# RWKV output projection by token groups in readout order, its first group with a pool and a bank of its own, in a two-layer hybrid backbone on one core

## Chip, cores and metric

The kernel runs on one core of one Trainium2 chip, as one launch. The metric is the device time of the launch in microseconds (us). The engines are named as in the profile: PE (TensorE matmul), PEld (its weight load), DVE (VectorE), ACT (ScalarE), POOL (GpSimd), SP (the engine that issues nearly all DMAs here). Each engine executes its own instructions in the order in which they stand in the program.

## What is computed

Two layers over 512 latent tokens of width 1024 and 256 context tokens. Layer 0 is grouped-query attention with a SwiGLU feed-forward, layer 1 a bidirectional RWKV-7 mixer with a SwiGLU feed-forward, then a final RMSNorm. The change lies in two places: where layer 0 begins, and between the RWKV scan and the last feed-forward. The reference of the latter, cut to what matters:

```python
mu = jnp.mean(wkv, axis=-1, keepdims=True)                # wkv: both scan directions added, (B, T, H, 64)
var = jnp.mean(jnp.square(wkv - mu), axis=-1, keepdims=True)
gn = ((wkv - mu) * lax.rsqrt(var + GN_EPS)).reshape(B, T, H * N) * ln_g + ln_b
bonus = sum(jnp.sum(r * k_d * r_k, axis=-1, keepdims=True) for k_d in k_dirs) * v
out = (gn + bonus.reshape(B, T, H * N)) * g               # g = sigmoid(...) @ g2
y = out @ wo
x = x + m[:, 2] * y
h2 = _rmsnorm(x, norm2_g[i]) * (1.0 + m[:, 4]) + m[:, 3]
x = x + m[:, 5] * _swiglu(h2, ffn_wg[i], ffn_wu[i], ffn_wd[i])
```

All products with large weights are done in three parts: operand and weight are split into a high part (a cast to fp32r) and a low part (the rest), and high·high, low·high and high·low are summed in PSUM.

## The kernel before

The program is written in a tile framework whose scheduler decides the order of the instructions on each engine from the code, the pools and the buffer counts. So a change in one stage can also turn the order in another.

The stages, in the profiled execution: layer 0 (its norm and the projection of queries, keys and values first), the RWKV projections, the scan in token chunks of 64 (roughly 1290 to 1784 us), the readouts, the output projection (1814 to 1860 us), the feed-forward (to about 2207 us), the final norm and the write of the output.

**The scan's loads.** For each head group and chunk, the scan's inputs are computed in an elementwise phase that loads `rt`, `kt`, `kk`, `AR`, `GA` (`L1034`, `L1096`, `L1097`) and writes `d_q`, `d_b`; the scan's steps load `Rb`, `T`, `Bs` (`L1269`, `L1245`, `L1256`). SP issues all of them in one row. An issue that waits for a free buffer holds up all issues behind it.

**Readouts.** `readout(g, i)` (`L1386` to `L1433`) is called for two head groups g = 0, 1 and i = 0 to 3. It handles 128 tokens, chunks 3-i and 4+i of the eight, since the forward and backward scans meet in the middle and give these chunks at the same time. It loads `yr` (the scan's results, `L1392`) and `vr` (`L1396`), adds the two directions (`L1401`), normalises (`L1403` to `L1414`, on DVE for g = 1), transposes `yr` and `vr` on PE (`pw`, `pvb`), multiplies tg by g2 on PE (`pgt`), and forms z and its high and low parts `oTh`, `oTl` (`L1427` to `L1433`). A call (g, 3) can begin only after the last scan step.

**Output projection.** `out_half` (`L264`) computes for half of the tokens (256 columns) the eight output tiles f: four blocks b, each loading two `wr` raws of 512 KB (`L249`) and covering f = 2b and 2b+1. For each f, two units `wu` (high part by ACT, `L239`; low part by DVE or POOL in turn, `L241`) give 24 matmuls `yps`; `add_gated` (`L258`, DVE) adds the result to `xT`, whose part is then written to `xd`. There are seven unit buffers (`UNITS`) and four raws (`RAWS`), shared by both halves and the feed-forward, and six PSUM banks for `yps`. The halves are tokens 0 to 255 and 256 to 511, so half 0 needs chunks 0 to 3, and thus every one of the eight readouts.

**Where layer 0 begins.** `xT` (tokens transposed, 3 MB) is built and written to `xd` by one DMA (`L560`) that stands on SP ahead of loads of `wraw` (weights of the first projection); modulation gives `tt`, `hh` (its high part, ACT `L558`), `hl` (its low part, DVE `L559`).

## Time and profile before

| | |
|---|---|
| three timed runs | 2244.11, 2254.23, 2256.9 us (median 2254.23) |
| the profiled execution | 2246.71 us |
| its span, first to last instruction | 2245.0 us |
| mean granted TensorE clock | 0.934 |
| PE busy | 2005.4 us (89% of the span) |
| DVE, ACT, POOL busy | 1638.5, 1138.0, 684.3 us |

The span and the time of the profiled execution differ by 1.7 us. The runs of one and the same program lie up to 12.8 us apart (0.6%). PE is busy nine tenths of the span, but the share differs much by stage, so that a change in a stage is read from that stage alone.

### The profile page before, as it was taken

Reading aid. Unit: us, or ns where it says so; the run is one execution under the profiler, and the core shown is the slowest. Engines: PE = TensorE matmul, PEld = TensorE weight load, DVE = VectorE, ACT = ScalarE, POOL = GpSimd, SP = SyncE. Lnnn points to the kernel's source line nnn. Section 1 sums busy time; section 2 is a strip of 40 time slices with the busy share of each in tenths; the row PEclk is TensorE's granted clock in tenths of the full one; section 3 lists DMA queues with packets and bytes.
Section 4 is the critical chain, followed back from the end, with each engine's and each line's share of the span. In section 5 each row is a group of like instructions: output and inputs, shape, how many; then the busy total and the mean of one; then the engine's idle time right before and its main releaser. Section 6 shows DMA issues by size and latency. Waiting matters only on the chain.

```text
span 2245.0 us, 43057 instructions
## 1 busy us (share of the span) xinstructions
PE 2005.4 (89%) x16566; PEld 1769.6 (79%) x16566; DVE 1638.5 (73%) x3119; ACT 1138.0 (51%) x2322; POOL 684.3 (30%) x564
## 2 busy tenths in 40 slices
PE   6998999898999999996988979766878687999998
PEld 4995555697999999995776957655767586899998
DVE  4565556668777677768566488699586678899997
ACT  5536566655333333335333665865765556444443
POOL 1120000126444434423133141221110415666661
PEclk7999999999999999997997989896999788999999
DMA  8106663353221222212226574774644654332331
GB/s 305 57 20 225 225 229 109 124 160 130 77 75 57 75 67 75 66 52 71 85 84 223 163 214 150 218 210 127 196 137 148 197 160 139 116 104 87 111 98 72
DMA packets 250076, 294.12 MB, mean 131 GB/s; under 512 B 36200, under 2 KB 176720, under 8 KB 249488
## 3 DMA queue, kind: packets, MB, share of 16 engines
q1 hardware_dynamic: 249152, 290.52, 41.8%
q8 instruction: 131, 2.15, 0.4%
q10 hardware_dynamic: 352, 0.60, 0.1%
q0 software_dynamic: 368, 0.26, 0.1%
q14 instruction: 73, 0.60, 0.1%
HBM read 228.40 MB, written 50.33 MB: 124 GB/s over the span
## 4 chain that ended last, share of the span: by engine, by line
PE 63%; DVE 15%; DMA 8%; issue 5%; ACT 4%; POOL 3%; SPq 1%; DVEq 0%; POOLq 0%; ACTq 0%
PE yps L445 13%; PE A L395 8%; PE B L395 5%; PE C L395 5%; PE yps L228 5%; PE po L747 3%; PE S L728 2%; PE PTp L742 2%; PE mps L126 2%; PE pj L228 2%; PE qps L595 2%; DVE wu L241 2%; PE qps L597 2%; PE qps L596 2%; PE pr L1337 2%
## 5 line engine op out<-in xcount | busy, mean ns | idle before, releaser
L445 PE MATMUL yps<-gh,wu 128*128 128x384 f32 (+2 forms) x1120 | 324.7, 346 | 0.0
L258 DVE SCALAR_TENSOR_TENSOR xT<-yps,modT,xT 128x384 f32<-128x384 f32 (+3 forms) x360 | 185.4, 537 | 125.6 <-PE yps L445 106.9
L239 ACT CAST wu<-wr 128x512 fp32r<-128x512 f32 x276 | 168.5, 620 | 172.0 <-PE A L395 55.9
L239 ACT CAST wu<-ws 128x512 fp32r<-128x512 f32 x176 | 109.2, 621 | 223.5 <-PE yps L445 62.1
L445 PEld LDWEIGHTS yps<-gh,wu 128*128 128x128 f32 x1120 | 202.5, 189 | 11.4
L241 POOL TENSOR_TENSOR wu<-wr,wu 128x512 fp32r<-128x512 f32 x86 | 123.3, 1434 | 236.1 <-ACT wu L239 212.4
L445 PE MATMUL yps<-gl,wu 128*128 128x384 f32 (+2 forms) x560 | 193.1, 345 | 0.0
L241 DVE TENSOR_TENSOR wu<-wr,wu 128x512 fp32r<-128x512 f32 x190 | 164.8, 872 | 14.5 <-ACT wu L239 14.1
L349 POOL TENSOR_TENSOR ws<-wr 128x512 f32<-128x512 f32 x88 | 129.5, 1477 | 147.7 <-DMA wr<-in_ffn_wg_dram 67.9
L241 DVE TENSOR_TENSOR wu<-ws,wu 128x512 fp32r<-128x512 f32 x111 | 138.3, 1247 | 20.8 <-ACT wu L239 20.7
L241 POOL TENSOR_TENSOR wu<-ws,wu 128x512 fp32r<-128x512 f32 x65 | 100.1, 1540 | 65.5 <-ACT wu L239 65.5
L228 PE MATMUL yps<-oTh,wu 128*128 128x384 f32 (+1 forms) x512 | 111.3, 309 | 1.1 <-ACT wu L239 1.0
L445 PEld LDWEIGHTS yps<-gl,wu 128*128 128x128 f32 x560 | 105.9, 189 | 4.3
L731 DVE TENSOR_REDUCE mx<-S 128x1 f32<-128x768 f32 (+1 forms) x96 | 74.7, 778 | 44.4 <-PE S L728 43.9
L1136 POOL TENSOR_SCALAR_AFFINE_SELECT GA<-GA 64x512 f32<-64x512 f32 x48 | 37.6, 783 | 199.4 <-ACT GA L1134 196.4
L395 PE MATMUL C<-x5h,wu 128*128 128x384 f32 (+1 forms) x352 | 85.2, 319 | 14.4 <-ACT x5h L312 12.3
L743 ACT COPY PT<-PTp 128x384 f32<-128x384 f32 (+1 forms) x160 | 69.4, 466 | 54.0 <-PE PTp L742 53.8
L742 PEld LDWEIGHTS PTp<-ident,pr 128*128 128x128 f32 x448 | 50.2, 144 | 50.4 <-issue 23.6
L395 PE MATMUL A<-x1h,wu 128*128 128x384 f32 (+1 forms) x352 | 83.0, 311 | 4.7 <-ACT wu L239 2.1
L228 PEld LDWEIGHTS yps<-oTh,wu 128*128 128x128 f32 x512 | 85.7, 189 | 1.9 <-ACT wu L239 1.4
L395 PE MATMUL B<-x2h,wu 128*128 128x384 f32 (+1 forms) x352 | 84.7, 309 | 1.2 <-POOL wu L241 1.2
L395 PE MATMUL A<-x6h,wu 128*128 128x384 f32 (+1 forms) x352 | 80.4, 310 | 4.1 <-ACT x6h L312 3.5
(408 smaller groups left out, 6251.3 us busy)
## 6 DMA issues: line engine op xcount, KB each, us to landing
mw<-in_mod_w_dram SPq DMA_DIRECT2D x48, 1024.0 KB, 5.3
wr<-in_ffn_wg_dram SPq DMA_DIRECT2D x44, 512.0 KB, 4.0
wr<-in_ffn_wu_dram SPq DMA_DIRECT2D x44, 512.0 KB, 3.9
wr<-in_ffn_wd_dram SPq DMA_DIRECT2D x44, 512.0 KB, 3.9
d_b<-BK SPq DMA_DIRECT2D x24, 512.0 KB, 3.8
Bs<-d_b SPq DMA_DIRECT2D x48, 256.0 KB, 3.5
wraw<-in_rwkv_wrkv_dram SPq DMA_DIRECT2D x32, 256.0 KB, 3.0
wr<-in_rwkv_wo_dram SPq DMA_DIRECT2D x16, 512.0 KB, 4.8
```

Source lines behind the costliest of these rows:

```text
L126: nc.tensor.matmul(ps[32 * g:32 * g + 32, :], sc[:, k, :], w[:, k - nk * i, :], start=(k < 4), stop=(k >= 4))
L228: nc.tensor.matmul(ps, w(k), x(k, sl), start=(k == 0 and i == 0), stop=(k == nk - 1 and i == 2))
L239: nc.scalar.copy(hi, raw)
L241: (nc.gpsimd if lane["n"] % 3 == 0 else nc.vector).tensor_tensor(out=lo, in0=raw, in1=hi, op=ALU.subtract)
L258: nc.vector.scalar_tensor_tensor(out=xT[:, f, t0:t1], in0=ps[:, t0 - sl.start:t1 - sl.start], scalar=modT[:, l, 8 * m + f, s:s + 1], in1=x ...
L349: nc.gpsimd.tensor_tensor(out=t, in0=x, in1=y, op=op)
L395: nc.tensor.matmul(ps, w[:, k], x[:, k], start=(k + j == 0), stop=(k == 3 and j == 2))
L445: nc.tensor.matmul(ps, u[k // 2][w][:, k % 2, fs], gs[k // 2][x][:, k % 2, sl], start=(k + j == 0), stop=(k == nk - 1 and j == 2))
L731: nc.vector.tensor_reduce(out=mx, in_=S[:, :nk * P], axis=AX.X, op=ALU.max)
L742: nc.tensor.transpose(ps[:, t - t0, :], pr_[:, P * t:P * t + P], ident)
L743: nc.scalar.copy(PT[h][:, t0:t1, P * qt:P * qt + P], ps[:, :t1 - t0, :])
L747: nc.tensor.matmul(po[HD * h:HD * h + HD, :], vt[:, k0 // P + t, HD * kv:HD * kv + HD], PT[h][:, t, :], start=(t == 0), stop=(t == nk - 1))
```

## The change

1. The output projection's halves are made of other tokens. `xT` is kept in the order of the readouts in layer 1: half 0 holds chunks 2, 3, 4, 5 (readouts i = 0 and 1 of both groups), half 1 the rest. `xT` and `tg` are loaded in three pieces each, and the output rows are written to their places at the end.
2. Half 0 gets a weight pool of its own, `fw0`, with two raws and three units instead of four and seven, and one PSUM bank, "A0", in which the two f of a block lie side by side. Half 1 keeps the old pool and the six banks. The readouts' `pgt` gives up bank "A0" and shares "z" with `pw`.
3. The PSUM pool of the scan is closed only after half 0; the buffers of the second half's normalised tokens and `fg` come later.
4. In layer 0, the write of `xT` to `xd` is two DMAs instead of one, and it stands behind an added DVE instruction that adds zero times the last `hl` to one column of `xT`.

```diff
 UNITS, RAWS = 7, 4
+FEW = (2, 3)
...
     def unit(wp, raw, shape):
-        u = wp.tile([P, 2, 512], F32R, name="wu", tag="u", bufs=UNITS)
+        u = wp.tile([P, 2, 512], F32R, name="wu", tag="u", bufs=FEW[1] if wp is few.get("wp") else UNITS)
...
-            raw = wp.tile([P, 4, 256], F32, name="wr", tag="r", bufs=RAWS)
+            raw = wp.tile([P, 4, 256], F32, name="wr", tag="r", bufs=FEW[0] if wp is few.get("wp") else RAWS)
...
-    def out_half(wp, pf, xT, src, xh, xl, l, m, sl, ready=None):
+    def out_half(wp, pf, xT, src, xh, xl, l, m, sl, ready=None, bank=None):
         tags = [f"{z}{y}" for z in "ABC" for y in range(2)]
         w = sl.stop - sl.start
         for b in range(4):
             rw_ = (ready or {}).get(b) or raws(wp, src, 256 * b, 256)
+            pair = pf.tile([P, 2, 256], F32, name="yps", tag=bank) if bank else None
             for q in range(2):
                 f = 2 * b + q
                 us = [unit(wp, r[:, :, P * q:P * q + P], (4, P)) for r in rw_]
-                ps = pf.tile([P, 512], F32, name="yps", tag=tags[f % 6])[:, :w]
+                ps = pair[:, q, :w] if bank else pf.tile([P, 512], F32, name="yps", tag=tags[f % 6])[:, :w]
...
-                nc.sync.dma_start(out=xd, in_=xT)
+
+                nc.vector.scalar_tensor_tensor(out=xT[:, :, 0:1], in0=hl[:, KT - 1:KT, 0:KT].rearrange("p o k -> p k o"), scalar=0.0,
+                                               in1=xT[:, :, 0:1], op0=ALU.mult, op1=ALU.add)
+                for k in range(0, KT, 4):
+                    nc.sync.dma_start(out=xd[:, k:k + 4], in_=xT[:, k:k + 4])
...
+    RUNS = ((0, 128, 256), (256, 0, 128), (384, 384, 128))
+    POS = (4, 5, 0, 1, 2, 3, 6, 7)
...
-            nc.sync.dma_start(out=tg, in_=d_g)
+        for z, t0, n in RUNS:
+            nc.sync.dma_start(out=tg[:, z:z + n], in_=d_g[:, t0:t0 + n])
...
-                pw, pvb, pg_ = (pE.tile([P, 4, P], F32, name=z, tag=t) for z, t in (("pw", "z"), ("pvb", "mg"), ("pgt", "A0")))
-                cks = slice(ck[0], ck[1] + 1, ck[1] - ck[0])
+            pw, pvb, pg_ = (pE.tile([P, 4, P], F32, name=z, tag=t) for z, t in (("pw", "z"), ("pvb", "mg"), ("pgt", "z")))
+            cks = slice(POS[ck[0]], POS[ck[1]] + 1, POS[ck[1]] - POS[ck[0]])
...
-            nc.sync.dma_start(out=xT, in_=xd[:, :, 0:L])
-            rdx.close()
-            pE_s.close()
-            hp = pool(wo, "hp")
-            n2 = L // 2
-            xv = {i: [hp.tile([P, 4, n2], F32R, name=f"x{i}{z}") for z in "hl"] for i in ORDER}
-            pf = pool(ff, "pf", 1, psum=True)
-            for th in range(2):
-                out_half(wp, pf, xT, a["rwkv_wo"][0], lambda k, sl: oTh[k // 4][:, k % 4, sl], lambda k, sl: oTl[k // 4][:, k % 4, sl], 1, 2,
-                         slice(n2 * th, n2 * th + n2))
-                norm_half(tp, pf, xT, th, 1, 1, xv, L)
+        for z, t0, n in RUNS:
+            nc.sync.dma_start(out=xT[:, :, z:z + n], in_=xd[:, :, t0:t0 + n])
+        for g in range(2):
+            for i in range(4):
+                readout(g, i)
+        few["wp"] = wp0 = pool(wo, "fw0")
+        heads = [lambda k, sl, z=z: z[k // 4][:, k % 4, sl] for z in (oTh, oTl)]
+        halves = [slice(0, n2), slice(n2, L)]
+        out_half(wp0, pE, xT, a["rwkv_wo"][0], *heads, 1, 2, halves[0], bank="A0")
+        pE_s.close()
+        pf = pool(ff, "pf", 1, psum=True)
+        norm_half(nt, pf, xT, 0, 1, 1, xv, L)
+        out_half(wp, pf, xT, a["rwkv_wo"][0], *heads, 1, 2, halves[1])
+        wo.close()
...
-                nc.sync.dma_start(out=out[P * i:P * i + P, :], in_=o)
+                t0 = (128, 256, 0, 384)[i]
+                nc.sync.dma_start(out=out[t0:t0 + P, :], in_=o)
```

**What the scheduler makes of it, first place.** PE between the scan's last matmuls and the projection, in the program before: `pw_18990`, `pw_19040`, `pw_19090`, `pw_19138` are the transposes of readouts (1,0), (1,1), (1,2), (1,3), and `yps_19195` is the projection's first tile.

```order
L1418 MATMUL pw_18990<-ident_60,yr_18964 128x128 x4
L1418 MATMUL pw_19040<-ident_60,yr_19014 128x128 x4
L1420 MATMUL pvb_19041<-ident_60,vr_19018 128x128 x4
L1422 MATMUL pgt_19042<-tg_18758,g2_18756 128x128 x4
L1420 MATMUL pvb_19091<-ident_60,vr_19068 128x128 x4
L1422 MATMUL pgt_19092<-tg_18758,g2_18756 128x128 x4
L1418 MATMUL pw_19090<-ident_60,yr_19064 128x128 x4
L1418 MATMUL pw_19138<-ident_60,yr_19114 128x128 x4
L1420 MATMUL pvb_19139<-ident_60,vr_19116 128x128 x4
L1422 MATMUL pgt_19140<-tg_18758,g2_18756 128x128 x4
L228 MATMUL yps_19195<-oTh_18751,wu_19189 128x256
```

The same place after the change; the four readouts of group 1 are `pw_18999`, `pw_19049`, `pw_19099`, `pw_19147`, and `yps_19178`, `yps_19247` are half 0's first two pairs. Where a line of dots stands, the rest of the 12 matmuls of a unit follows.

```order
L1430 MATMUL pw_18999<-ident_60,yr_18973 128x128 x4
...
L1430 MATMUL pw_19049<-ident_60,yr_19023 128x128 x4
...
L1430 MATMUL pw_19099<-ident_60,yr_19073 128x128 x4
L229 MATMUL yps_19178<-oTh_18750,wu_19182 128x256
...
L1434 MATMUL pgt_19101<-tg_18762,g2_18760 128x128 x4
L1432 MATMUL pvb_19148<-ident_60,vr_19125 128x128 x4
L229 MATMUL yps_19178<-oTh_18755,wu_19211 128x256
...
L1430 MATMUL pw_19147<-ident_60,yr_19123 128x128 x4
L229 MATMUL yps_19247<-oTh_18755,wu_19248 128x256
...
L1434 MATMUL pgt_19149<-tg_18762,g2_18760 128x128 x4
```

Before, all eight readouts stand ahead of the first `yps`. After, half 0's first 48 matmuls (four units of 12) stand ahead of the last transpose `pw_19147`, and 24 more between it and the last `pgt`; 120 of half 0's 192 and all 192 of half 1 follow.

**Second place.** SP between the scan's last loads and the projection, before. `wr_19185` to `wr_19397` are the raws of half 0 in the order of its blocks, `yr_19064` and `yr_19114` the loads of readouts (1,2) and (1,3).

```order
L249 DMA wr_19185<-in_rwkv_wo_dram 128x4x256
L249 DMA wr_19187<-in_rwkv_wo_dram 128x4x256
L249 DMA wr_19255<-in_rwkv_wo_dram 128x4x256
L1396 DMA vr_19068<-d_v_10403 64x512 x2
L249 DMA wr_19257<-in_rwkv_wo_dram 128x4x256
L249 DMA wr_19325<-in_rwkv_wo_dram 128x4x256
L249 DMA wr_19327<-in_rwkv_wo_dram 128x4x256
L1392 DMA yr_19064<-d_y_10404 128x512
L249 DMA wr_19395<-in_rwkv_wo_dram 128x4x256
L1392 DMA yr_19114<-d_y_10404 128x512
```

After: `wr_19174` and `wr_19176` are half 0's first block, `wr_19527` to `wr_19599` raws of half 1, `wr_19243` and `wr_19245` half 0's second block, `yr_19073` and `yr_19123` the loads of readouts (1,2) and (1,3).

```order
L251 DMA wr_19527<-in_rwkv_wo_dram 128x4x256
L1408 DMA vr_19027<-d_v_10405 64x512 x2
L1404 DMA yr_19023<-d_y_10406 128x512
L251 DMA wr_19529<-in_rwkv_wo_dram 128x4x256
L251 DMA wr_19597<-in_rwkv_wo_dram 128x4x256
L251 DMA wr_19599<-in_rwkv_wo_dram 128x4x256
L1408 DMA vr_19077<-d_v_10405 64x512 x2
L251 DMA wr_19243<-in_rwkv_wo_dram 128x4x256
L1404 DMA yr_19073<-d_y_10406 128x512
L251 DMA wr_19245<-in_rwkv_wo_dram 128x4x256
...
L1404 DMA yr_19123<-d_y_10406 128x512
```

Four raws of half 1 now stand ahead of half 0's second block, and the load of readout (1,1), `yr_19023`, stands behind three raws; before, it was ahead of all of them. DVE's row follows suit: eight low parts of units stand ahead of the last transpose's source instead of four.

**Third place.** SP in the scan, at the loads for the last group of chunks, before: `AR0`, `d_b5`, `kk`, `rt_17333` are the elementwise phase's, `Rb1`, `T`, `Bs` those of a scan step.

```order
L1269 DMA Rb1_13739<-d_q3_11681 64x256
L1245 DMA T_16630<-d_v_10403 64x512
L1317 DMA d_y_10404<-y_15937 128x512
L1245 DMA T_16630<-d_v_10403 64x512
L1269 DMA Rb1_13739<-d_q3_11681 64x256 x3
L1256 DMA Bs_16762<-d_b3_11675 128x512 x2
L1096 DMA AR0_11687<-lw_16424 64x512 x2
L1104 DMA d_b5_11677<-BK_17251 256x4x128
L1034 DMA kk_17309<-d_kk_10400 128x512
L1034 DMA rt_17333<-d_r_10401 128x512
```

After:

```order
L1103 DMA AR0_11689<-lw_16426 64x512 x2
L1104 DMA GA_17254<-lw_16426 64x512
L1111 DMA d_b5_11679<-BK_17253 256x4x128
L1041 DMA kk_17311<-d_kk_10402 128x512
L1041 DMA rt_17335<-d_r_10403 128x512
L1104 DMA GA_17342<-lw_17229 64x512 x2
L1054 DMA wa0_11691<-in_rwkv_w2_dram 64x128
L1054 DMA wa0_11691<-in_rwkv_a2_dram 64x128
L1041 DMA kt_17420<-d_k_10401 128x512
L1276 DMA Rb1_13741<-d_q3_11683 64x256
```

The elementwise phase's loads have moved ahead of a scan step's. The code of the scan is not touched by the diff.

## Rows read from the trace of the kernel before

**Rows 1.** The page's head and its busy time by engine.

```profile
span 2245.0 us, 43057 instructions
PE 2005.4 (89%) x16566; PEld 1769.6 (79%) x16566; DVE 1638.5 (73%) x3119; ACT 1138.0 (51%) x2322; POOL 684.3 (30%) x564
```

**Rows 2.** Busy time by stretch: PE, PEld, DVE, ACT, POOL, clock, DMA share, GB/s.

```profile
1780.00:1800.00 20.00, 9.30 (x103) 7.95 (x102) 18.34 (x32) 10.89 (x24) 6.40 (x5) 0.67 0.82 249
1800.00:1820.00 20.00, 13.77 (x89) 13.03 (x89) 15.37 (x33) 9.66 (x23) 1.05 (x2) 0.78 0.16 44
1840.00:1860.00 20.00, 19.97 (x176) 19.78 (x175) 17.51 (x39) 15.36 (x36) 6.71 (x5) 1.00 0.64 190
```

**Rows 3.** Chain of waits, readouts into projection: start us, us, what.

```profile
1786.92 6.05 DMA wr<-in_rwkv_wo_dram
...
1809.55 0.70 DVE yr L1414
1810.39 1.09 PE pw L1418 x4
...
1812.33 1.71 PE pgt L1422 x8
1814.04 23.86 PE yps L228 x204
```

**Rows 4.** Groups of instructions between 1784 and 1816 us.

```profile
L1433 DVE TENSOR_TENSOR oTl<-z,oTh 128x512 fp32r<-128x512 f32 x6 | 4.1, 684 | 0.7 <-ACT oTh L1432 0.7
L239 ACT CAST wu<-wr 128x512 fp32r<-128x512 f32 x7 | 4.0, 616 | 3.2 <-DMA wr<-in_rwkv_wo_dram 3.2
L241 POOL TENSOR_TENSOR wu<-wr,wu 128x512 fp32r<-128x512 f32 x3 | 4.0, 1327 | 3.8 <-ACT wu L239 3.8
L241 DVE TENSOR_TENSOR wu<-wr,wu 128x512 fp32r<-128x512 f32 x4 | 2.7, 685 | 0.6 <-ACT wu L239 0.6
```

**Rows 5.** SP's issues, readouts: start us, us, queue, line, transfer, count.

```profile
1782.88 2.80 SPq L249 DMA_DIRECT2D wr<-in_rwkv_wo_dram  x3
...
1786.92 6.49 SPq L249 DMA_DIRECT2D wr<-in_rwkv_wo_dram  x3
1796.43 0.34 SPq L1392 DMA_DIRECT2D yr<-d_y  x1
...
1799.30 0.34 SPq L1392 DMA_DIRECT2D yr<-d_y  x1
```

**Rows 6.** DMA issues, 1715 to 1820 us: size, median us to landing.

```profile
wr<-in_rwkv_wo_dram SPq DMA_DIRECT2D x8, 512.0 KB, 4.8
yr<-d_y SPq DMA_DIRECT2D x15, 256.0 KB, 3.5
```

**Rows 7.** The gated adds of the projection: ns min/median/max, first and last start.

```profile
L258 DVE SCALAR_TENSOR_TENSOR xT<-yps,modT,xT x16: 472/482/486, 1818.8 to 1862.9; 128x256 f32<-128x256 f32 x16
```

**Rows 8.** PE's timeline: last matmuls of the scan and of the projection.

```profile
1783.44 0.28 PE L1311 MATMUL py<-S,Rb 128*64 128x64 f32 x2
...
1859.47 0.28 PE L228 MATMUL yps<-oTh,wu 128*128 128x256 f32 x1
```

**Rows 9.** DVE's timeline at the projection's end.

```profile
1860.38 0.68 DVE L241 TENSOR_TENSOR wu<-wr,wu 128x512 fp32r<-128x512 f32 x1
...
1862.86 0.47 DVE L258 SCALAR_TENSOR_TENSOR xT<-yps,modT,xT 128x256 f32<-128x256 f32 x1
```

**Rows 10.** ACT's timeline where layer 0 begins; in brackets idle time and releaser.

```profile
46.18 0.59 ACT L128 COPY mev<-mps 128x512 f32<-128x512 f32 x1 [0.97 <-PE mps L126]
...
55.40 1.04 ACT L218 CAST whi<-wraw 128x1024 fp32r<-128x1024 f32 x1
```

**Rows 11.** Chain of waits where layer 0 begins.

```profile
46.18 0.59 ACT mev L128
46.82 1.87 PE mps L131 x8
```

**Rows 12.** DMA issues, 0 to 60 us.

```profile
mw<-in_mod_w_dram SPq DMA_DIRECT2D x8, 1024.0 KB, 13.6
xd<-xT SPq DMA_DIRECT2D x1, 3072.0 KB, 18.8
```

**Rows 13.** Chain of waits in the scan.

```profile
1611.78 7.40 DMA rt<-d_r
...
1627.19 2.98 DMA rt<-d_r
```

**Rows 14.** SP's issues in the scan.

```profile
1599.20 0.56 SPq L1047 DMA_DIRECT2D wa<-in_rwkv_a_dram  x1
1602.83 0.45 SPq L1269 DMA_DIRECT2D Rb<-d_q  x1
...
1610.96 0.73 SPq L1034 DMA_DIRECT2D kk<-d_kk  x1
```

130 lines of the change are left out of this document (67 added, 63 removed).

## The prediction

> **What bounds the kernel now.** I read the page first, then the chain of waits, then the two stages that the diff touches by stretches, engine by engine. PE is busy 2005.4 of 2245.0 us [rows 1], so most of the kernel is bound by matmuls whose number does not change. A gain must come from stretches in which PE stands idle. One of these is the passage from the scan to the projection: between 1780 and 1800 us PE is busy 9.30 of 20 us, at a mean granted clock of 0.67, and between 1800 and 1820 us 13.77 us, while DVE is busy 18.34 and 15.37 us [rows 2]. The chain shows why. It goes from a raw of weights (6.05 us) through DVE to the last readout's transpose at 1810.39, its pgt at 1812.33, and then the first yps at 1814.04 [rows 3]. From there PE is full: 204 yps in 23.86 us, 0.117 us each [rows 3], and 19.97 of 20 us before the end [rows 2]. The last yps starts at 1859.47 [rows 8] and ends its share of the array at 1859.6. So the stage consists of a part bound by DVE and DMA (the readouts, to 1810.4) and a part bound by PE (two halves of 192 matmuls, 22.5 us each).
>
> **The change, part by part.** The sum is made against the profiled execution, 2246.7 us (span 2245.0 [rows 1] and 1.7 around it). The four known times of this program (2244.1, 2246.7, 2254.2, 2256.9) have the mean 2250.5, so that a median of new runs is looked for 3.8 us above the sum.
>
> *Work moved ahead of the readouts' end.* Half 0 no longer needs readouts (·,2) and (·,3). The order shows how much the scheduler makes of it: 48 of half 0's matmuls stand ahead of the last transpose, 48 x 0.117 = 5.6 us. Another 24 stand between that transpose and the last pgt, where before PE waited for nothing but its own transposes. What remains behind the last transpose is 144 matmuls of half 0 (16.9 us) and 192 of half 1 (22.5 us).
>
> *What the readouts pay.* DVE has hardly a gap between 1780 and 1800 us [rows 2], and in its row the changed program puts eight low parts of units ahead of the last transpose's source instead of four, and one gated add. Four times 0.685 [rows 4] and 0.48 [rows 7] give 3.2 us. SP puts raws of half 1 ahead of the loads of readouts (1,1), (1,2) and (1,3). A raw of 512 KB at the 249 GB/s of this stretch [rows 2] takes 2.1 us. Readout (1,1)'s load falls behind three raws; before, the six raws went out between 1782.88 and 1793.41 and the two late readout loads at 1796.43 and 1799.30, with little behind them [rows 5]. A readout load lands 3.5 us after its issue, a raw 4.8 us [rows 6]. I take one raw, 2.1 us, as the delay that DVE sees; the bounds are 0 (the load lands while DVE is at the added low parts) and three raws, 6.3. So the last transpose comes at 1810.4 + 3.2 + 2.1 = 1815.7 instead of 1810.4.
>
> *What half 0 pays for one bank.* With the two f of a block in one bank, PE's first matmul of an f waits until the gated add of the f before it has read the bank; before, six banks left PE no such wait. One gated add takes 0.482 us [rows 7]; with the events around it I estimate 0.6 us for each of the six f behind the last transpose, 3.6 us. The bounds are 0 (weights are later anyway, so the wait is inside theirs) and 1.2 us each, 7.2 us, when DVE is at a low part (0.685 [rows 4]) as the bank falls due. The Trainium skill, PSUM — Partial Sum Buffer, section "PSUM bank collisions raise a hardware error", says that PSUM has to be guarded by bank and quadrant and not by address. By that rule the two f of a pair cannot overlap although they use different columns, which speaks against this change; no row of the kernel before shows it, since there every f had its own bank.
>
> *Sum for this stage.* 1815.7, its transposes 1.1, 144 matmuls 16.9, one pgt (half of the 1.71 for two [rows 3]) 0.9, bank waits 3.6, half 1 22.5: 1860.7 against 1859.6, so **+1.1 us**. The bounds: nothing late and no bank waits gives 1851.8, -7.8; all upper ends give 1815.7 + 4.2, and 3.6 more for the bank, +8.9.
>
> *After the last yps.* DVE reaches the last gated add only at 1862.86, 3.3 us after PE is done, because low parts of the next stage stand ahead of it [rows 9]. Half 1 has seven of its sixteen units made early, so DVE, busy 17.51 of 20 us in this stretch [rows 2], is a little less behind. I take **-1.0**, between 0 and -2.4 (3.3 less the add itself and its event). The feed-forward's own order is as before and counts nothing.
>
> *Layer 0.* The 3 MB write to xd took 18.8 us to land in a queue in which the mw loads took 13.6 [rows 12]. Taken out of their way, the next wraw lands earlier, and the scheduler uses that: two casts of whi, 1.04 us each, now stand on ACT ahead of the copy mev at 46.18, before which ACT had 0.97 us of idle time [rows 10]. The copy is on the chain, followed by PE's mps [rows 11]. 2.08 - 0.97 = **+1.1 us**. Below: the casts are work that ACT no longer has later, and the mw loads come earlier, -1; above: all of 2.1. The added DVE instruction handles 8 elements a partition and counts nothing. The write, now behind the last hl, is hidden under the matmuls of the first projection; without that cover it would hold up the loads behind it for up to its 18.8 us [rows 12].
>
> *The scan, which the diff does not touch.* The chain waits 7.40 us and 2.98 us for rt [rows 13]. SP had stood still from 1599.76 to 1602.83 at an Rb of a scan step, and kk and rt went out only at 1610.96 and 1611.78, behind that step's loads [rows 13, 14]. After, they stand ahead of that Rb. That can take away most of the 10.4 us; but it puts some nine issues of about 0.65 us ahead of the step's loads, 5.9 less the 3.07 us that SP stood idle, so the scan step may be 2.8 us later. When rt is on time, DVE or the scan step is late next. I take **-2.0**, from -8 to +3. Small turns of order elsewhere in the scan are without a sign that I can read.
>
> *The split loads* of xT and tg run under the scan and are counted at nothing; PE's own work there covers them.
>
> Sum: +1.1 - 1.0 + 1.1 - 2.0 = -0.8, 2245.9 us for an execution like the profiled one, **2249.7** on the scale of the four times. I predict 2250.
>
> **The rivals.** *Faster: the moved matmuls are really free.* If the loads land under DVE's work and the bank waits fall into waits for weights, the stage gives -7.8, and with an rt on time (-6) and -1 at the end the time is 2250.5 - 14.8 = 2235.7. For it: PE idles some 17 us between 1780 and 1820 [rows 2]. Against it: DVE, which sets the readouts' pace, gets more to do just there.
>
> *Slower: two raws and three units starve half 0.* The next block's first raw can be loaded only after this block's third unit is made from the last but one. Load 4.8 [rows 6], cast 0.62 and low part 1.33 on POOL [rows 4] make 6.7 us, of which two stocked units of 1.4 us of matmuls cover 2.8; 4.0 us for each of three blocks is 12.0, in which the 3.6 of the bank are contained, so +8.4 on the forecast: 2258. With the readouts late by two more raws (4.2) it is 2262. It decides when a block takes more than 9.6 us instead of 5.6. For it: the first projection weights were waited for already with four raws (ACT 3.2 us [rows 4]). Against it: those waits fell together with readout loads, which are over by then.
>
> *The layer-1 change does nothing and the scan's order decides.* Then the time moves by -8 to +3 as above, 2242 to 2253, inside the forecast's range.
>
> **How the numbers follow.** About 0.5%, 11 us, is what a measurement of this kernel can tell from no change. The forecast, with the third rival, lies within it: chance 0.58, its own range 2242 to 2258. The faster rival gets 0.23; slower 0.19. The range of 8 in 10 reaches into both: 2239 to 2262.
>
> **What would show it.** Right: in the changed profile yps stand between pw and pgt before 1816 us; the last pw at about 1816; PE idle in front of yps for some 0.6 us per f, released by DVE's xT; the last yps near 1861 if the scan ends as before; mev about 1 us later. Wrong: the last pw before 1811, or PE waits above 2 us for ACT's wu in half 0; an end of the scan that is over 8 us from 1783.7 [rows 8]; a shift in the feed-forward, whose rows I take as unchanged.

## The result, and the profile after

The changed kernel takes 2258.62 us (median of 18 runs, 2254.32 to 2267.48), the kernel before 2245.5 us (18 runs on the same chips): a ratio of 1.0056, with a 95% interval from 1.0043 to 1.0069. It is slower, by some 13 us. The number lies inside the range predicted, but the case forecast as likeliest, no change that can be measured, did not come.

The page's head after the change, which answers to [rows 1]:

```profile
span 2259.1 us, 43028 instructions
PE 2015.3 (89%) x16566; PEld 1779.1 (79%) x16566; DVE 1633.8 (72%) x3120; ACT 1136.6 (50%) x2322; POOL 688.8 (30%) x564
```

PE has as many matmuls as before and DVE a little less to do, and yet PE is busy 9.9 us longer; the profiled spans differ by 14.1 us. So time was lost in two ways: PE waited, and it ran the same matmuls more slowly. Busy time by stretch, in the columns of [rows 2]:

```profile
1780.00:1800.00 20.00, 9.82 (x44) 8.54 (x44) 18.22 (x26) 12.09 (x26) 8.10 (x6) 0.60 1.05 315
1800.00:1820.00 20.00, 14.40 (x81) 13.13 (x82) 15.55 (x37) 9.03 (x22) 2.32 (x2) 0.63 0.20 59
```

Half 0's matmuls do stand among the readouts now, and yet PE is hardly busier there (9.82 and 14.40 us against 9.30 and 13.77). These stretches are fixed in time, though, and the scan ended 7.4 us sooner here. So the same from mark to mark: from behind the scan's last matmul to the last transpose `pw`, and from there to the last `yps` of the projection, after the change:

```profile
1776.29:1818.15 41.86, 24.39 (x127) 21.64 (x126) 36.29 (x65) 19.99 (x43) 9.51 (x7) 0.63 0.62 185
1818.15:1869.90 51.75, 44.64 (x362) 43.45 (x361) 31.17 (x62) 26.93 (x59) 12.08 (x9) 0.97 0.41 124
```

and before:

```profile
1783.65:1810.39 26.74, 9.81 (x59) 8.30 (x57) 25.13 (x52) 13.62 (x30) 7.45 (x6) 0.71 0.62 183
1810.39:1859.60 49.21, 49.21 (x413) 49.21 (x414) 37.16 (x69) 31.68 (x67) 13.19 (x10) 0.95 0.59 176
```

In the first stretch PE stood idle for 17.5 us after the change and for 16.9 before. The change put 48 of half 0's matmuls into it, and also matmuls of one more readout, which before had run ahead of the scan's end; the stretch grew by as much as they took, and PE's idle time did not shrink. In the second stretch, where PE was full before, it stands idle for 7.1 us. Over both PE is busy 69.0 us instead of 59.0, which is the longer busy time of the page's head. The mean granted clock of the first stretch is 0.63, and the 48 matmuls moved into it took 9.34 us there, 0.195 each instead of 0.117 [rows 3].

PE's timeline through the readouts into half 0 (in brackets idle time and what ended it):

```profile
1776.08 0.28 PE L1318 MATMUL py<-S,Rb 128*64 128x64 f32 x2
...
1780.18 0.63 PE L1430 MATMUL pw<-ident,yr 128*128 128x128 f32 x4 [1.34 <-DVE z L1441]
1782.40 2.08 PE L1434 MATMUL pgt<-tg,g 128*128 128x128 f32 x8 [1.59 <-ACT z L1439]
...
1789.60 0.63 PE L1430 MATMUL pw<-ident,yr 128*128 128x128 f32 x4 [1.80 <-DVE yr L1426]
1792.78 2.08 PE L1434 MATMUL pgt<-tg,g 128*128 128x128 f32 x8 [2.54 <-ACT z L1439]
...
1803.36 1.09 PE L1430 MATMUL pw<-ident,yr 128*128 128x128 f32 x4 [5.50 <-DVE yr L1426]
1806.04 2.07 PE L1434 MATMUL pgt<-tg,g 128*128 128x128 f32 x8 [1.59 <-ACT z L1439]
...
1818.15 0.60 PE L1430 MATMUL pw<-ident,yr 128*128 128x128 f32 x4
1818.98 0.36 PE L229 MATMUL yps<-oTh,wu 128*128 128x256 f32 x1 [0.23 <-DVE xT L260]
...
1826.58 0.36 PE L229 MATMUL yps<-oTh,wu 128*128 128x256 f32 x1 [0.86 <-DVE xT L260]
...
1837.82 0.36 PE L229 MATMUL yps<-oTh,wu 128*128 128x256 f32 x1 [3.52 <-DVE xT L260]
...
1869.80 0.28 PE L229 MATMUL yps<-oTh,wu 128*128 128x256 f32 x1
```

Three things are to be seen. First, `pgt` now waits for ACT's z, three times (1.59, 2.54 and 1.59 us), and a `pw` for DVE's z (1.34 us): with `pw` and `pgt` in one bank, `pgt` begins only when ACT has read `pw` out of it, and the next `pw` only when DVE has multiplied by `pgt`. The transposes of readouts (1,0) and (1,1), at 1789.60 and 1803.36, now stand 13.8 us apart. Before, it was 2.9 us:

```profile
1795.31 1.08 PE L1418 MATMUL pw<-ident,yr 128*128 128x128 f32 x4 [8.01 <-DVE rs_y L161]
1798.18 1.09 PE L1418 MATMUL pw<-ident,yr 128*128 128x128 f32 x4 [1.79 <-DVE yr L1414]
```

Such a delay is handed on through the loads. `yr` has two buffers, so readout (1,3) loads into the one that (1,1) used, and SP issues that load only behind (1,1)'s transpose: 28 us behind the scan's last matmul, where it was 16 us [rows 5].

```profile
1804.48 0.34 SPq L1404 DMA_DIRECT2D yr<-d_y  x1
```

Second, the last `pw` stands 42 us behind the scan's last matmul, before 27 us [rows 3, 8]. Third, half 0's tiles wait for the gated add (`xT`, L260) that reads the one bank. For that third wait, the sums over the stretch from 1818 to 1870 us (PE's waits: us in total, times, longest):

```profile
PE yps L229 <- DVE xT L260: 6.4, 6, 3.5
PE yps L229 <- POOL wu L243: 0.7, 1, 0.7
```

The longest of them on the chain of waits (start, us, what):

```profile
1830.66 5.18 DMA wr<-in_rwkv_wo_dram
...
1835.93 0.63 ACT wu L241
...
1836.59 0.07 DVE wu L243
...
1837.19 0.49 DVE xT L260
...
1837.82 2.34 PE yps L229 x13
```

The gated add that frees the bank is ready long before, but on DVE it stands behind a low part, which waits for ACT's high part, which waits for a raw: pool and bank are tied together by DVE's order. And PE pays once more for standing idle. Three stretches (columns as above):

```profile
1834.40:1838.60 4.20, 0.78 (x6) 0.81 (x7) 2.01 (x4) 1.56 (x3) 0.89 (x1) 1.00 0.19 65
1838.60:1842.40 3.80, 3.80 (x20) 3.61 (x18) 0.01 (x1) 0.62 (x1) 1.27 (x1) 0.55 0.09 31
1842.40:1847.00 4.60, 3.47 (x29) 3.40 (x29) 1.40 (x3) 0.66 (x2) 0.00 (x0) 1.00 0.10 32
```

Behind the idle time the granted clock stands at 0.55, close to the lower of its two levels (1.2 of 2.4 GHz), and 20 matmuls take 3.80 us, 0.19 each instead of 0.117.

Last, ACT behind the projection, before:

```profile
1866.37 1.28 ACT L158 ACT_TABLE_LOAD   x1
1867.66 0.26 ACT L158 ACTIVATE rs_y<-rbp,epst 128x2 f32<-128x2 f32 x1
1868.99 0.62 ACT L239 CAST wu<-ws 128x512 fp32r<-128x512 f32 x1 [1.06 <-POOL ws L349]
```

and after:

```profile
1880.41 0.62 ACT L241 CAST wu<-ws 128x512 fp32r<-128x512 f32 x1 [4.10 <-POOL ws L352]
1881.04 1.28 ACT L159 ACT_TABLE_LOAD   x1
1882.34 0.26 ACT L159 ACTIVATE rs_y<-rbp,epst 128x2 f32<-128x2 f32 x1
```

The square root of half 1's norm (`rs_y`) has gone behind a cast of the feed-forward's weights that waits 4.10 us for POOL.

### The profile page after: what moved, and what is told of

It is laid out like the page before. It is cut to its first block, busy times and chain, and to the rows that moved or that the text cites. A ratio compares the mean times of both kernels' runs of the same rounds, so it can differ in the third digit from the quotient of the medians.

```text
span 2259.1 us, 43028 instructions
## 1 busy us (share of the span) xinstructions
PE 2015.3 (89%) x16566; PEld 1779.1 (79%) x16566; DVE 1633.8 (72%) x3120; ACT 1136.6 (50%) x2322; POOL 688.8 (30%) x564
## 3 DMA queue, kind: packets, MB, share of 16 engines
q1 hardware_dynamic: 251664, 290.52, 41.4%
## 4 chain that ended last, share of the span: by engine, by line
PE 61%; DVE 15%; DMA 9%; issue 6%; ACT 5%; POOL 3%; SPq 1%; DVEq 0%; POOLq 0%; ACTq 0%
PE yps L448 12%; PE A L398 7%; PE B L398 5%; PE C L398 5%; PE yps L229 4%; PE po L754 3%; PE S L735 2%; PE PTp L749 2%; PE pj L229 2%; DVE wu L243 2%; PE mps L127 2%; PE qps L602 2%; PE qps L604 2%; PE qps L603 2%; DMA wr<-in_ffn_wu_dram 2%
## 5 line engine op out<-in xcount | busy, mean ns | idle before, releaser
L260 DVE SCALAR_TENSOR_TENSOR xT<-yps,modT,xT 128x384 f32<-128x384 f32 (+3 forms) x360 | 185.4, 537 | 128.1 <-PE yps L448 106.7
L229 PE MATMUL yps<-oTh,wu 128*128 128x384 f32 (+1 forms) x512 | 117.2, 318 | 8.2 <-DVE xT L260 6.4
L1143 POOL TENSOR_SCALAR_AFFINE_SELECT GA<-GA 64x512 f32<-64x512 f32 x48 | 41.4, 862 | 189.7 <-ACT GA L1141 182.2
L229 PEld LDWEIGHTS yps<-oTh,wu 128*128 128x128 f32 x512 | 89.0, 196 | 10.2 <-ACT wu L241 5.1
```

Source lines behind the costliest of these rows:

```text
L229: nc.tensor.matmul(ps, w(k), x(k, sl), start=(k == 0 and i == 0), stop=(k == nk - 1 and i == 2))
L260: nc.vector.scalar_tensor_tensor(out=xT[:, f, t0:t1], in0=ps[:, t0 - sl.start:t1 - sl.start], scalar=modT[:, l, 8 * m + f, s:s + 1], in1=x ...
```

## Where the time lies, by stage

All in us, read from the timeline of each kernel's profile: the start of the scan's last `py`; from there to the last transpose `pw`; to the last `yps` of the projection; to PE's spreading of the norm factors of half 1 (a small matmul behind `rs_y`); to the last `yps` of the feed-forward; to the end. The two columns on the right say how many of the projection's 384 `yps` stand ahead of the last `pw`, and how long PE stood idle from the scan's last `py` to the projection's last `yps`.

| kernel | scan ends | to last pw | to last yps | to spread | feed-forward | to end | span | yps ahead | PE idle |
|---|---|---|---|---|---|---|---|---|---|
| before | 1783.5 | 27.6 | 48.4 | 10.8 | 359.1 | 15.6 | 2245.0 | 0 | 16.9 |
| after | 1776.1 | 42.4 | 51.3 | 16.9 | 357.0 | 15.4 | 2259.1 | 48 | 24.6 |
| e9 (before, shared z) | 1775.5 | 37.5 | 52.4 | 11.3 | 356.2 | 15.6 | 2248.5 | 0 | 23.1 |
| e8 (own banks, shared pool) | 1774.7 | 41.7 | 35.1 | 17.9 | 361.6 | 15.4 | 2246.4 | 123 | 16.6 |
| e11 (after, root first) | 1781.5 | 39.7 | 51.5 | 9.9 | 363.2 | 15.3 | 2261.1 | 48 | 23.0 |
| e10 (e8, root first) | 1779.3 | 43.7 | 34.2 | 9.9 | 361.2 | 15.4 | 2243.7 | 123 | 15.6 |

After less before: -7.4 + 14.8 + 2.9 + 6.1 - 2.1 - 0.2 = +14.1. The feed-forward's last `yps` is at 2229.4 in the kernel before, not at the 2207 given among the stages at the start.

The last `pw` is not the same mark in every kernel, since work that stood behind it can stand ahead of it. Where kernels differ in that, compare the sum of the columns to the last `pw` and to the last `yps`, that is from the scan's end to the last `yps` of the projection: 76.0 us before, 93.7 after, 89.9 in e9, 76.8 in e8, 91.2 in e11, 77.9 in e10.

A row is one execution. The end of the scan moves by some 10 us from one to the next: with layer 0's write as before it came at 1775.5 in e9 and at 1786.7 in e2, with the changed write at 1774.5 in e1 and at 1784.3 in r13. But what lies behind it repeats: 461.5 and 461.7 us for before and e1, which have the same code there, and 483.0, 481.3 and 481.6 us for after, e2 and e4, whose code there is nearly the same. So the change costs some 20 us behind the scan's end, more than the 13 us by which the runs differ. Whether the rest is won ahead of that mark, no run here shows. Verdicts below go by the medians of runs, and the stages only say where.

## The experiments

Each ratio is to the kernel before, run on the same chip, with its 95% interval. It is the ratio on record, and the quotient of the two medians can differ from it by up to 0.14% (e7: 1.0035 instead of 1.0049).

### Which of the places

**e1_write_only**: before, with layer 0's write of xd alone as in the change.

```diff
-                nc.sync.dma_start(out=xd, in_=xT)
+                nc.vector.scalar_tensor_tensor(out=xT[:, :, 0:1], in0=hl[:, KT - 1:KT, 0:KT].rearrange("p o k -> p k o"), scalar=0.0,
+                                               in1=xT[:, :, 0:1], op0=ALU.mult, op1=ALU.add)
+                for k in range(0, KT, 4):
+                    nc.sync.dma_start(out=xd[:, k:k + 4], in_=xT[:, k:k + 4])
```

> The kernel before with the later write of xT in layer 0 alone; the readouts and the projection stay as before. In the program its scan has the order of loads of the changed kernel. Theory 1 (the write's place turns the scan's order, and the scan's gain is real): the scan's last matmul comes near 1776 instead of 1783.5, as in the changed kernel. If the gain is passed on, about 7 us faster than before, 2238. Theory 2 (the readouts are paced by their loads and by DVE, not by the end of the scan): the scan ends near 1776 all the same, but the last transpose stays near 1810 and the time within 2 us of before, 2244 to 2247. Rival (the scan's gain comes from the split loads or the pools of layer 1): scan end at 1783, no change of time.

2245.5 us, 0.9995 [0.9981, 1.0008]: nothing. This program has the changed order of the scan, and in its profile the scan ended at 1774.5, yet its runs take as long as before: the profiled execution, 2237.95 us, was the fastest of its twelve.

**e2_layer1_only**: the change with layer 0's write as before.

```diff
-                nc.vector.scalar_tensor_tensor(out=xT[:, :, 0:1], in0=hl[:, KT - 1:KT, 0:KT].rearrange("p o k -> p k o"), scalar=0.0,
-                                               in1=xT[:, :, 0:1], op0=ALU.mult, op1=ALU.add)
-                for k in range(0, KT, 4):
-                    nc.sync.dma_start(out=xd[:, k:k + 4], in_=xT[:, k:k + 4])
+                nc.sync.dma_start(out=xd, in_=xT)
```

> The changed kernel with the write of xT as before; all edits of layer 1 stay. Theory 1: the scan ends near 1783 again, and if its gain had been passed on in the changed kernel the time is 7 us above it, 2266. Theory 2: the readouts' own pace decides, time 2258 to 2260. Rival (the write is what costs): back near 2246.

2262.41 us, 1.0072 [1.0052, 1.0092]. The whole loss is layer 1's.

**e4_fg_late**: the change, with the load of `fg` behind the feed-forward.

```diff
-        nc.scalar.dma_start(out=fg, in_=a["final_g"].rearrange("(l f) -> l f", l=1).to_broadcast([P, D]))
...
+        nc.scalar.dma_start(out=fg, in_=a["final_g"].rearrange("(l f) -> l f", l=1).to_broadcast([P, D]))
```

> The changed kernel with the load of fg (the final norm's gain, 512 KB) issued after the last feed-forward instead of between the halves' norms. Theory (this load collides with the feed-forward's first raws, which is the 4 us that the stretch after the last yps of the projection grew): 3 to 4 us faster than the changed kernel, 2255. Rival (that stretch grew since ACT's square root now stands behind a cast that waits for the feed-forward's raws, whatever fg does): within 1 us of the changed kernel.

2258.7 us, 1.0059 [1.0038, 1.0079], the spread as late as in the changed kernel (17.6 us behind the last `yps`): the theory that this load holds ACT up fell.

### One scarcity undone

**e3_shared_pool**: half 0 takes its weights from the old pool.

```diff
-        few["wp"] = wp0 = pool(wo, "fw0")
+        wp0 = wp
```

> The changed kernel, but half 0 takes its weights from the old pool of four raws and seven units, which both halves then share; one bank for its outputs as in the change. Theory A (the small pool starves half 0): the 144 matmuls behind the last transpose take near 22 us instead of 28.6, and half 1's raws no longer stand ahead of half 0's; 6 us faster than the changed kernel, 2252. Theory B (readouts delayed by the projection's work on DVE and in the queue): last transpose stays 7 to 8 us later than before, at about 1817, and 0 to 3 us are gained. Both may hold: then 2250 or lower.

2261.97 us, 1.0072 [1.0053, 1.0090]. Readouts and projection were 10.0 us shorter (38.3 and 45.4 us), the feed-forward 7.1 us longer; the runs show no gain, where 6 us were expected.

**e6_larger_pool**: half 0's own pool with four raws and five units.

```diff
-FEW = (2, 3)
+FEW = (4, 5)
```

> The changed kernel with four raws and five units in half 0's own pool instead of two and three. Theory A: half 0's 144 matmuls behind the last transpose take 22 to 24 us instead of 28.6, and 4 to 6 us are gained on the changed kernel, 2253 to 2255, since the feed-forward's own pool is left alone. Rival (the bank's waits and DVE's adds set the pace of half 0, not the weights): within 2 us of the changed kernel.

2263.1 us, 1.0064 [1.0044, 1.0083]. The waits for the gated add fell from 6.4 to 3.5 us, the longest from 3.5 to 0.8 us; the time did not fall.

**e5_two_banks**: the two f of a block in banks "A0" and "A" (two buffers).

```diff
-            pair = pf.tile([P, 2, 256], F32, name="yps", tag=bank) if bank else None
...
-                ps = pair[:, q, :w] if bank else pf.tile([P, 512], F32, name="yps", tag=tags[f % 6])[:, :w]
+                ps = pf.tile([P, 512], F32, name="yps", tag=tags[f % 6])[:, :w] if not bank else (pf.tile([P, 512], F32, name="yps", tag="A", bufs=2) if q else pf.tile([P, 512], F32, name="yps", tag=bank))[:, :w]
```

> The changed kernel with half 0's tiles in three banks in turn (A0, and the two of the scan's tag A) instead of a pair in one; pgt still shares z, the pool stays small. If the one bank costs half 0 its waits: the 0.7 to 0.9 us of idle time ahead of each f are gone, from the last transpose to the last yps 47 to 48 us instead of 51.3, and 3 to 4 us faster than the changed kernel. If the raws of the small pool set the pace: the same 51 us and no change.

2258.99 us, 1.0044 [1.0029, 1.0059]. No wait for the gated add is left, and the last `pw` to the last `yps` takes 41.2 instead of 51.3 us, with 77 `yps` ahead of that `pw` instead of 48 (from the scan's end to the last `yps` 84.3 instead of 93.7 us); the feed-forward took 362.4 instead of 357.0.

**r15_z_undone**: `pgt` no longer shares z's bank, but takes the two banks of the scan's tag "A".

```diff
-            pw, pvb, pg_ = (pE.tile([P, 4, P], F32, name=z, tag=t) for z, t in (("pw", "z"), ("pvb", "mg"), ("pgt", "z")))
+            pw, pvb, pg_ = (pE.tile([P, 4, P], F32, name=z, tag=t, bufs=2 if t == "A" else None) for z, t in (("pw", "z"), ("pvb", "mg"), ("pgt", "A")))
```

> The changed kernel with pgt in the scan's two banks of tag A instead of in z; one bank for half 0's pairs and the small pool stay. If the shared z is an addend of its own: from the scan's end to the last transpose 33 to 37 us instead of 42.4, and 6 to 10 us faster than the changed kernel, ratio to before 0.999 to 1.002. If the small pool and the raws of half 1 ahead of the readouts' loads are the next bound: the last transpose stays beyond 39 us, and the ratio above 1.003, as with own banks alone.

2260.72 us, 1.0062 [1.0046, 1.0079]. To the last `pw` it took 36.0 us instead of 42.4, with 24 `yps` ahead of it instead of 48, and from there to the last `yps` 55.3 instead of 51.3, with 7.8 us of waits for the gated add. Over both only 2.4 us are gained.

### One scarcity alone

**e9_shared_z**: before, with `pgt` in the bank of `pw`; one word of the program.

```diff
-                pw, pvb, pg_ = (pE.tile([P, 4, P], F32, name=z, tag=t) for z, t in (("pw", "z"), ("pvb", "mg"), ("pgt", "A0")))
+                pw, pvb, pg_ = (pE.tile([P, 4, P], F32, name=z, tag=t) for z, t in (("pw", "z"), ("pvb", "mg"), ("pgt", "z")))
```

> The kernel before with one edit: pgt shares bank z with pw, as in the changed kernel, instead of having bank A0. Theory Z (the shared bank makes each readout wait: pw, then ACT's z, then pgt, then DVE's product, and only then the next pw; this is what set the readouts back by 13 to 15 us after the scan): from the scan's end to the last transpose 35 us or more instead of 28, and 6 to 12 us slower than before. Theory W (the weight units' casts and low parts ahead of the readouts set them back): no more than 2 us slower, since this kernel makes as many units early as before.

2257.66 against 2248.76 us, 1.0047 [1.0029, 1.0065], from this one word. What PE waited for in the readouts, before (1783 to 1814 us):

```profile
PE pw L1418 <- DVE rs_y L161: 8.0, 1, 8.0
PE pw L1418 <- DVE yr L1414: 6.3, 3, 2.7
PE pgt L1422 <- DVE z L1429: 2.6, 2, 1.7
```

and in e9 (1775 to 1815 us):

```profile
PE pgt L1422 <- ACT z L1427: 10.2, 5, 3.8
PE pw L1418 <- DVE rs_y L161: 5.2, 1, 5.2
PE pw L1418 <- DVE yr L1414: 4.6, 2, 3.3
PE pw L1418 <- DVE z L1429: 1.6, 2, 1.3
```

Two new waits, 10.2 and 1.6 us, stand against 2.6 that is gone and 4.5 less in the two rows that remain; up to the last `yps` PE stands idle for 23.1 us instead of 16.9. Before, `pgt` was made while ACT and DVE were at z, and now it follows ACT. They are the same two waits as in the profile after, and the transposes of readouts (1,0) and (1,1) stand as far apart as there, 13.7 us:

```profile
1787.51 1.09 PE L1418 MATMUL pw<-ident,yr 128*128 128x128 f32 x4 [3.34 <-DVE yr L1414]
1801.19 1.09 PE L1418 MATMUL pw<-ident,yr 128*128 128x128 f32 x4 [5.20 <-DVE rs_y L161]
```

**e7_own_banks**: the change, with `pgt` back in "A0" and half 0's pairs in two banks of their own, in turn. Of the three scarcities the small pool is left.

```diff
-            pair = pf.tile([P, 2, 256], F32, name="yps", tag=bank) if bank else None
+            pair = pf.tile([P, 2, 256], F32, name="yps", tag=bank, bufs=2) if bank else None
...
-            pw, pvb, pg_ = (pE.tile([P, 4, P], F32, name=z, tag=t) for z, t in (("pw", "z"), ("pvb", "mg"), ("pgt", "z")))
+            pw, pvb, pg_ = (pE.tile([P, 4, P], F32, name=z, tag=t) for z, t in (("pw", "z"), ("pvb", "mg"), ("pgt", "A0")))
...
-        out_half(wp0, pE, xT, a["rwkv_wo"][0], *heads, 1, 2, halves[0], bank="A0")
+        out_half(wp0, pE, xT, a["rwkv_wo"][0], *heads, 1, 2, halves[0], bank="A")
```

> The changed kernel with pgt back in bank A0, and half 0's pairs in the two banks of the scan's tag A in turn. Small pool and early weights of half 1 stay. Theory Z: the last transpose returns to within 4 us of before's distance from the scan's end (about 31), and the time to 2246 to 2250. Theory W: the distance stays near 40 us and the time above 2255.

2256.64 us, 1.0049 [1.0027, 1.0071]. The last transpose did not return to 31 us, as theory Z had it, but stands 41.4 us behind the scan's end, now with 96 `yps` ahead of it. The transposes of (1,0) and (1,1) are 3.6 us apart again.

**e8_own_banks_shared_pool**: the edit of e7, and with it that of e3. None of the three scarcities is left; half 0 still runs by the order of the readouts.

```diff
-        few["wp"] = wp0 = pool(wo, "fw0")
+        wp0 = wp
```

> As own banks, and half 0 takes its weights from the old pool of four raws and seven units, too. Theory Z with theory A (small pool starves half 0): the best of all, the last yps of the projection within 2 us of before or earlier, 2240 to 2247 unless the stretch behind the projection grows as it did with the shared pool alone (396.8 us instead of 385.5), then 2250.

2250.05 against 2248.76 us, 1.0007 [0.9997, 1.0017]: the time of before. The loss is explained by the three; the order itself brings nothing either. From the last `pw` to the last `yps` it takes 13.3 us less (35.1 against 48.4), because 123 `yps` stand ahead of that `pw` and not behind it; the `pw` comes 14.1 us later for it. From the scan's end to the last `yps` it is 76.8 us against 76.0, and PE's idle time 16.6 against 16.9.

### The late square root

**e11_root_first**: the change, with a small operation on POOL that makes the feed-forward's first weight sum wait for the norm's factor, so that ACT takes the square root first.

```diff
+            if l == 1:
+                few["rr"] = r
...
+                if "rr" in few:
+                    rr = few.pop("rr")
+                    nc.gpsimd.tensor_tensor(out=t[:, 0, 0:1], in0=rr[:, 0:1], in1=rr[:, 1:2], op=ALU.add)
```

> The changed kernel with one added small POOL instruction: the feed-forward's first weight sum waits for the second half's norm factor, so that ACT's square root stands ahead of the cast of that sum, as in the kernel before. Theory R (ACT's order delays the second half's norm): from the projection's last yps to PE's spread of the norm factors 11 us instead of 17, and 3 to 6 us faster than the changed kernel. Rival (the feed-forward is paced by the making of its weights on DVE and POOL, and what the norm gains is lost there): the 17 become 11, but the time stays within 2 us of the changed kernel.

2261.56 against 2249.23 us, 1.0047 [1.0033, 1.0061]. From the last `yps` to the spread 9.9 us instead of 16.9, as meant, but the feed-forward takes 363.2 instead of 357.0: 6.2 of 7.0 us are given back. Waits in e11 over the 60 us from the spread on:

```profile
ACT wu L241 <- POOL ws L357: 10.9, 4, 6.0
POOL wu L243 <- ACT wu L241: 8.1, 5, 4.8
POOL ws L357 <- DMA wr<-in_ffn_wu_dram: 7.5, 2, 5.7
```

The feed-forward's opening waits for its own weights: ACT for POOL's sum, POOL for the load. A sooner start meets later weights. That tells where the gains of e3 and e5 may have gone too; for those it is argued from the stage's length, not shown by an edit.

### Together, and the best version

**e10_banks_pool_root**: e8, and with it the edit of e11.

```diff
+            if l == 1:
+                few["rr"] = r
...
+                if "rr" in few:
+                    rr = few.pop("rr")
+                    nc.gpsimd.tensor_tensor(out=t[:, 0, 0:1], in0=rr[:, 0:1], in1=rr[:, 1:2], op=ALU.add)
```

> Own banks and the old, shared pool, and the square root first. Theory R: 4 to 6 us faster than own banks with the shared pool, that is 3 to 5 us faster than the kernel before (ratio near 0.998). Rival (paced by the feed-forward's weights): within 2 us of own banks with the shared pool, ratio 0.999 to 1.002.

2244.9 against 2249.23 us, 0.9980 [0.9966, 0.9994], the fastest kernel here: faster than the change, and by 0.2% than before, which is less than the 0.5% set in the prediction, and the next kernels, hardly different, do not repeat it.

**e12_banks_larger_pool_root**: e10 with a pool of its own for half 0 again, but four raws and five units.

```diff
-FEW = (2, 3)
+FEW = (4, 5)
...
-        wp0 = wp
+        few["wp"] = wp0 = pool(wo, "fw0")
```

> Own banks, an own pool of four raws and five units for half 0, and the square root first. If the small pool was what own banks alone lacked: the projection as short as with the shared pool (about 77 us from the scan's end to the last yps), and the old pool free for half 1 and the feed-forward, so 0 to 3 us better than with the shared pool. If raws of half 1 ahead of the readouts' loads set the readouts back: the projection 3 to 6 us longer than with the shared pool.

2249.52 us, 1.0001 [0.9988, 1.0015]. A pool of its own costs nothing that can be told; one too small does (e7 against e8).

**r14_one_bank_alone**: e10 with half 0's pairs in one bank again, "A0"; `pgt` goes to the two banks of tag "A" for that.

```diff
-            pair = pf.tile([P, 2, 256], F32, name="yps", tag=bank, bufs=2) if bank else None
+            pair = pf.tile([P, 2, 256], F32, name="yps", tag=bank) if bank else None
...
-            pw, pvb, pg_ = (pE.tile([P, 4, P], F32, name=z, tag=t) for z, t in (("pw", "z"), ("pvb", "mg"), ("pgt", "A0")))
+            pw, pvb, pg_ = (pE.tile([P, 4, P], F32, name=z, tag=t, bufs=2 if t == "A" else None) for z, t in (("pw", "z"), ("pvb", "mg"), ("pgt", "A")))
...
-        out_half(wp0, pE, xT, a["rwkv_wo"][0], *heads, 1, 2, halves[0], bank="A")
+        out_half(wp0, pE, xT, a["rwkv_wo"][0], *heads, 1, 2, halves[0], bank="A0")
```

> The fastest version so far (own banks, shared pool, root first), but with half 0's pairs in the one bank A0 and pgt in the two banks of tag A. The one bank costs half 0 its waits: 0.6 to 0.9 us for each of up to eight f, 3 to 6 us from the last transpose to the last yps, ratio to the fastest version 1.001 to 1.003; if the feed-forward's opening gives it back, within 2 us of the fastest version.

2254.61 against 2248.04 us, 1.0032 [1.0018, 1.0045], where the four kernels with two banks (e10, e12, r13, r16) lie at 0.9980 to 1.0006. PE's waits in r14, up to the projection's last `yps`:

```profile
PE pgt L1439 <- DVE z L1446: 3.7, 3, 2.2
PE yps L229 <- DVE xT L260: 3.0, 4, 1.2
```

and in e10:

```profile
PE yps L229 <- DVE xT L260: 1.4, 1, 1.4
PE pgt L1439 <- DVE z L1446: 0.6, 1, 0.6
```

From the scan's end to the last `yps` r14 takes 85.3 us instead of 77.9, but only 1.6 us of that are waits for the one bank; 3.1 are waits of `pgt` in its new place, and the order of the readouts has turned too (48 `yps` ahead of the last `pw` instead of 123). So the 0.3 to 0.5% are the price of the whole edit. What the one bank costs by itself is not shown.

**r13_low_parts_on_pool**: e10, with the low parts of half 0's first six units on POOL instead of DVE.

```diff
-        (nc.gpsimd if lane["n"] % 3 == 0 else nc.vector).tensor_tensor(out=lo, in0=raw, in1=hi, op=ALU.subtract)
+        few["pool"] = few.get("pool", 0) - 1
+        (nc.gpsimd if lane["n"] % 3 == 0 or few["pool"] >= 0 else nc.vector).tensor_tensor(out=lo, in0=raw, in1=hi, op=ALU.subtract)
...
+        few["pool"] = 6
```

> The fastest version so far with the low parts of half 0's first six units all on POOL instead of two of three on DVE. If DVE's work sets the readouts back: the last transpose 3 to 5 us sooner after the scan than the 43.7 of the fastest version, and the last yps 2 to 4 us sooner. If the weights' landing and the loads' order set them: no change, or up to 3 us later, since POOL takes 1.33 us for a low part where DVE takes 0.69.

2249.51 us, 1.0006 [0.9991, 1.0021]. Three low parts instead of eight stand on DVE ahead of the last transpose's source, which is ready 3.4 us sooner (37.0 us behind the scan's end instead of 40.4). The last `pw` comes 4.3 us sooner (39.4 us), but 85 `yps` stand ahead of it instead of 123, and the last `yps` comes only 1.6 us sooner (76.3 instead of 77.9). The feed-forward was 5.4 us longer.

**r16_old_write**: e10 with layer 0's write as before.

```diff
-                nc.vector.scalar_tensor_tensor(out=xT[:, :, 0:1], in0=hl[:, KT - 1:KT, 0:KT].rearrange("p o k -> p k o"), scalar=0.0,
-                                               in1=xT[:, :, 0:1], op0=ALU.mult, op1=ALU.add)
-                for k in range(0, KT, 4):
-                    nc.sync.dma_start(out=xd[:, k:k + 4], in_=xT[:, k:k + 4])
+                nc.sync.dma_start(out=xd, in_=xT)
```

> The fastest version so far with the write of xT in layer 0 as before, which also gives the scan its old order of loads. If the scan's order is worth what the two profiles seemed to show, 5 to 7 us slower than the fastest version; if those profiles differed by the variation from execution to execution, within 2 us of it, as the write alone changed nothing.

2248.25 us, 0.9996 [0.9980, 1.0011]; with e1 a second time, the write is worth nothing that can be told.

## Why the prediction was wrong, step by step

**The step that failed: "What the readouts pay".** It counted the added low parts and the late loads, 5.3 us, and had no term for `pgt` in the bank of `pw`, although the list of the change names it. The last `pw` came 14.8 us later behind the scan instead of 5.3 (at 1818.15 where 1815.7 was forecast, with the scan over 7.4 us sooner). Alone in the kernel before, the shared bank costs 0.47% (e9), by itself most of the 0.56%. The trace of the kernel before would have raised it: behind the last `pw` [rows 3] `pgt` began at 1812.12, while ACT was at z from 1811.57 to 1813.08; with both in one bank it must wait. Of the 5.3 us, the part for low parts (3.2) is borne out: eight did stand ahead, and r13 gives 3.4 for five of them. The late load of (1,3) did come, but behind a transpose that held its buffer, not behind raws in the queue. A delay by the raws' loads was not taken away by itself.

**"Work moved ahead of the readouts' end": it was not free.** The sum took 48 matmuls, 5.6 us, off what follows the last `pw` and put nothing ahead of it. They took 9.34 us there, at the lower granted clock, and PE's idle time up to the last `pw` did not fall (17.5 against 16.9). In e9, with the shared bank and nothing moved, it is 20.7: by these two executions some 3 of the 9.34 us found idle time, and the rest made the stretch longer.

**"What half 0 pays for one bank": right in mechanism, mis-sized.** Forecast 3.6 us in six waits, bounds 0 and 7.2; measured 6.4 us in six (the last of them, 0.47, at half 1's first tile), 3.5 of them one wait in which DVE stood at a low part without its raw. From the last `pw` on, half 0 took 28.6 us instead of the 22.5 of the sum: 6.4 and 0.7 us of waits where 3.6 were counted, and 1.5 us more for the matmuls at the lower clock behind the long wait; 1.1 us is not accounted for.

**The slower rival, "two raws and three units starve half 0".** Its time, 2258, is what came, by luck: its price is not where it put it. It named waits of 4.0 us in each of three blocks; the trace shows one of 3.5, and the rest of the loss has other causes. Yet the small pool does cost: with the banks undone, e7 is at 1.0049 and e8 without the pool at 1.0007.

**The bank rule.** The Trainium skill, PSUM — Partial Sum Buffer, section "PSUM bank collisions raise a hardware error", has PSUM guarded by bank and quadrant and not by address. The prediction weighed it for the two f of a pair, and the trace agrees as far as it goes: two of the six waits, 0.67 us each, stand within a pair, where PE waits for the reader of the other f although the columns differ. The other four stand where the next pair takes over the bank or half 1 begins. Whether the chip or the framework's guard asks for it, no run here tells. The prediction did not weigh it for `pgt` and `pw`, where it cost more.

**The three do not add.** e9 and e7 have one each, r14 one and another place for `pgt`: 0.3 to 0.5%. All three: 0.56%. Taking one away from three (e3, e5, e6, r15) leaves 0.4 to 0.7%. An explanation that fits, but is argued and not shown: they serve one passage in which the slowest sets the pace, and the opening of the feed-forward takes part of a gain back.

**"After the last yps": -1.0 forecast, wrong in sign.** DVE reaches the last gated add at 1872.82, 3.0 us behind the last `yps`, where it was 3.4 [rows 8, 9]: 0.4 gained, and the spread came 6.1 us later, since "the feed-forward's own order is as before" does not hold on ACT. Only 0.8 of e11's 7.0 us were kept, so this is no cause of much weight while the other waits stand; in e10 against e8 the sign is a gain, 0.9980 against 1.0007, but e12, r13 and r16, which have the root first too, lie at 0.9996 to 1.0006.

**Layer 0 (+1.1) and the scan (-2.0): nothing that can be told.** `mev`, late by 1 us in the forecast, was not late: it stands at 45.61 after the change and 46.18 before [rows 10]. The scan ended 7.4 us sooner in this one execution, but e1 has its order and its runs are no faster.

**The faster rival's free matmuls** were not found. In e8, where nothing is scarce, the 13.3 us that are gone behind the last transpose stand ahead of it: its source is ready on DVE 38.9 us behind the scan's end instead of 26.7, and PE stands idle as long as before (16.6 against 16.9). The rival's own counter-argument, that DVE sets the readouts' pace and gets more to do just there, is what this looks like; no run takes it apart.
